# Weights times values of the samples' attention: f32 matmuls against float32r matmuls of split operands

## The chip, the cores and the metric

The kernel runs on one core of a Trainium2 chip. The metric is the device time of one execution in microseconds, as the median of several runs; lower is better. Before the change it is 2456.01 us (three runs, 2455.13 to 2456.61). One further execution was taken by the hardware profiler; the views below are of that one.

The core has five engines that run their own instruction queues in order and wait for each other through semaphores: TensorE (PE, matmuls and transposes; PEld is its loading of the stationary operand), VectorE (DVE), ScalarE (ACT), GpSimd (POOL) and SyncE (SP, which here only issues transfers). Matmul results go to PSUM, everything else lies in SBUF or in HBM.

## What is computed

One layer of a hybrid decoder, for a prompt of 512 tokens and for 8 samples with 4 new tokens each. Both go through a wide input projection, an mLSTM branch, a sliding-window attention branch, a gated merge and a layer norm. The change touches only the attention of the samples, in the reference:

```python
def _swa_sample(q, k_new, v_new, k_buf, v_buf, slopes, sinks):
    k_all = jnp.concatenate([k_buf.astype(k_new.dtype), k_new], axis=1)
    v_all = jnp.concatenate([v_buf.astype(v_new.dtype), v_new], axis=1)
    ...
    out = _sink_attend(q, k_all, v_all, dist, valid, slopes, sinks)
...
# in _sink_attend
    p = jax.nn.softmax(jnp.concatenate([s, sink], axis=-1), axis=-1)[..., :-1]
    return jnp.einsum('...hgqk,...khd->...qhgd', p.astype(v.dtype), v)
```

For each sample there are 128 old keys and values and 4 new ones, 4 key/value heads of 64 and 32 query heads. So for one sample the weights are a matrix of 128 rows (32 heads times 4 tokens) by 132 keys, and the last einsum multiplies them by the values, 128 + 4 rows of 4 x 64 columns.

## The kernel before

**The main work.** The kernel is a long row of matrix products of weights with the 544 tokens (512 of the prompt, 32 of the samples). In the stretch around the change the function paired does them: two column blocks of 128 at a time, in seven steps (half_product, lines 686 to 696), each of 24 float32r matmuls with 272 columns, about 3 us. A product of f32 accuracy is made of three float32r ones: the operand is split into a high part, which is the value rounded to float32r, and a low part, the rest; then high times high, high times low and low times high are added up in PSUM. For the weights, split (lines 202 to 211) makes the high half wh by a cast on ScalarE (L208) and the low half wl by a subtraction on VectorE (L209); there are two buffers of each, and paired prepares them some steps ahead. Sums of raw weights that the seven-step scheme needs come from VectorE as well (L674), and gather (L698 to 723) takes the finished banks out of PSUM.

**The side work.** Everything else is written as generators. After each step tick() lets every live generator run to its next yield, so its instructions are placed between two steps of the main work. The order on each engine comes from a scheduler that simulates the instructions' times at build time (schedule_with_timeline_sim); tc.issue_after pins an instruction behind another one on its engine, and high_priority moves the weight splits ahead.

**The samples' attention** is such a generator, sample_attention (L983 to 1115). It runs after the prompt's attention and before the samples' mLSTM heads, one yield for a step:

- Tiles are taken from the pools t1 and t2 (L984 to 996), with one buffer for each tag. A tile whose tag is used again waits until all uses of the earlier one are over.
- Loads on SyncE's queue: the queries qraw, the new keys kas, the old keys kb (1 MB, L1003), then the new values vas (32 rows of 256, L1007), the old values vb (1 MB, L1008), and the gates gas (L1015). VectorE scales the queries into qas (L1012).
- keysT (L1017 to 1026) turns the old keys on TensorE (L1022) and ScalarE copies them to the tiles with the tags kT0 and kT1 (L1024). The score matmuls (L1039, L1040) follow, then VectorE adds the bias into E (L1042, L1044), and ScalarE takes the exponentials (L1052). E holds for each sample 128 rows by 128 + 4 weights.
- The 4 weights of the new tokens are copied to En (L1059), a tile that GpSimd has set to zero (L995), so that sample b has 32 columns there of which only its own four are filled. En for one sample, turned, is 32 rows (all samples' new tokens) by 128, and fits vas, which holds the new values of all 32 tokens.
- weightsT (L1063 to 1076) turns, for two samples at a time, E (L1068) and En (L1069) on TensorE; ScalarE copies the first (L1073), VectorE the second (L1074), into a tile PT of plain f32.
- values_of (L1078 to 1101) multiplies: for each of the two samples a matmul of PT with vb (L1083, 128 rows) and one of the 32 rows with vas (L1084), both plain f32, both 256 columns into the same PSUM region. VectorE then scales the rows into O (L1090), TensorE turns O (L1095), and VectorE multiplies by the gates (L1101). Four such groups run, the weights of the next one being turned right after the matmuls of the one before (L1103 to 1112).

Of the kernel before, what the change touches and what calls it, by code (L numbers as in the profile page):

```python
# [15 lines left out]
F32 = mybir.dt.float32  # L16
F32R = mybir.dt.float32r
AF = mybir.ActivationFunctionType
ALU = mybir.AluOpType

D = 2048
SEQ = 512
NB = 8
NTS = 4
NS = NB * NTS
T = SEQ + NS
# [5 lines left out]
GRP = 8  # L32
# [42 lines left out]
def _build(tc, nc, i, o, es):  # L75
# [12 lines left out]
    V, A, G, PE = nc.vector, nc.scalar, nc.gpsimd, nc.tensor  # L88
# [16 lines left out]
    def nm(s):  # L105
        count[0] += 1
        return f"{s}_{count[0]}"
# [9 lines left out]
    def r32(ap):  # L117
        return ap.bitcast(F32)
# [33 lines left out]
    ident = cc[:, C_ID:C_ID + 128]  # L152
# [20 lines left out]
    d_vr = dr.tile([T, 256], F32, name="d_vr")  # L173
# [136 lines left out]
    for c0, n in ((0, 256), (256, 256), (512, 512), (1024, 512), (1536, 512)):  # L310
        if c0 < 1536:
            t_ = xr.tile([128, 4, n], F32, tag=f"x{n}", name=nm("xr"))[:]
        else:
            t_ = act2.tile([128, 8, HT], F32, tag="act", name=nm("xr"))[:].rearrange("p a b -> p (a b)")
            t_ = blk(t_[:, 0:4 * n])
# [16 lines left out]
    for g in range(8):  # L332
        for q in range(2):
            k = g * 2 + q
            pt = sm()
# [11 lines left out]
            else:  # L347
                hilo(pt[:], xk2[0][k // 4 - 2][:, k % 4, 0:SEQ], xk2[1][k // 4 - 2][:, k % 4, 0:SEQ])
                x_cast = state["x_cast"]
                c = (slice(None), k - 8, slice(0, SEQ - HT))  # L350
                state["x_end"] = V.tensor_tensor(out=s1r[c], in0=pt[:, HT:SEQ], in1=s1r[c], op=ALU.subtract)
        if g % 2:
# [8 lines left out]
            else:  # L361
                hilo(src, *(xk2[p][g // 2 - 2][:, :, SEQ:T] for p in range(2)))
                c = (slice(None), slice(k4.start - 8, k4.stop - 8), slice(SEQ - HT, HT))
# [619 lines left out]
    def sample_attention():  # L983
        t1, t2 = pool(esT, "t1", 1), pool(esT, "t2", 1)  # L984
        gas = t1.tile([128, 16, NS], F32, name="gas")
        qraw = t1.tile([128, 2, GRP, NS], F32, name="qraw")
        qas = t1.tile([128, 2, NB, GRP, NTS], F32, name="qas")
        kas = t1.tile([128, 2, NS], F32, name="kas")
        vas = t1.tile([32, 256], F32, name="vas")
        kb = t1.tile([128, NB, 256], F32, name="kb")  # L990
        vb = t1.tile([128, NB, 256], F32, name="vb")
        E = t1.tile([128, NB, 132], F32, name="E")

        En = t1.tile([128, 9 * NS], F32, name="En")
        G.memset(En[:], 0.0)  # L995
        st = t1.tile([128, 4, NB], F32, name="sast")
        def buffer_load(t_, src):
            nc.sync.dma_start(t_[:], i[src].rearrange("b t k d -> t b (k d)"))

        with tc.issue_after(state["load"].ins):  # L1000
            nc.sync.dma_start(qraw[:], d_qa[:])
            nc.sync.dma_start(kas[:], d_ka[:, :, SEQ:T].rearrange("k p t -> p k t"))
            buffer_load(kb, "state_attn_k")  # L1003
        yield
        yield
        with tc.issue_after(state["load"].ins):
            nc.sync.dma_start(vas[:], d_vr[SEQ:T])  # L1007
            buffer_load(vb, "state_attn_v")  # L1008
        yield
        with tc.issue_after(state["split"].ins):  # L1010
            for j in range(2):
                V.tensor_scalar(qas[:, j], qraw[:, j].rearrange("p g (b t) -> p b g t", t=NTS), 0.125, None, op0=ALU.mult)  # L1012
        yield
        with tc.issue_after(state["load"].ins):
            nc.sync.dma_start(gas[:], d_bra[:, :, SEQ:T].rearrange("k p t -> p k t"))  # L1015

        def keysT(b2_):  # L1017
            kTs = []
            for bb in range(2):
                pk = sm()  # L1020
                for kk in range(2):
                    PE.transpose(pk[:, kk * 128:kk * 128 + 128], kb[:, b2_ * 2 + bb, kk * 128:kk * 128 + 128], ident)  # L1022
                kT = t1.tile([128, 2, 128], F32, tag=f"kT{bb}", name=nm("kT"))
                A.copy(kT[:].rearrange("p a b -> p (a b)"), pk[:, 0:256])  # L1024
                kTs.append(kT)
            return kTs

        kTs = keysT(0)
        for b2_ in range(4):
            yield  # L1030
            ps_, pn_ = sm(), sm()
            for bb in range(2):
                b = b2_ * 2 + bb
                for kvh in range(KVH):
                    r = slice((kvh % 2) * 64, (kvh % 2) * 64 + 64)
                    q = qas[r, kvh // 2, b].rearrange("p g t -> p (g t)")
                    orow = slice(kvh * 32, kvh * 32 + 32)
                    tp = ((kvh % 2) * 64, kvh * 32)
                    PE.matmul(ps_[orow, bb * 128:bb * 128 + 128], q, kTs[bb][r, kvh // 2], start=True, stop=True, tile_position=tp)  # L1039
                    PE.matmul(pn_[orow, bb * 4:bb * 4 + 4], q, kas[r, kvh // 2, b * 4:b * 4 + 4], start=True, stop=True, tile_position=tp)  # L1040
            sl = slice(b2_ * 2, b2_ * 2 + 2)
            V.tensor_tensor(out=E[:, sl, 0:128], in0=blk(ps_[:, 0:256], 2),  # L1042
                            in1=state["ca"][:, 256:384].unsqueeze(1).to_broadcast([128, 2, 128]), op=ALU.add)
            V.tensor_tensor(out=E[:, sl, 128:132], in0=blk(pn_[:, 0:8], 2),  # L1044
                            in1=state["ca"][:, 384:388].unsqueeze(1).to_broadcast([128, 2, 4]), op=ALU.add)
            if b2_ < 3:
                kTs = keysT(b2_ + 1)
        V.tensor_reduce(st[:, 0], E[:], mybir.AxisListType.X, ALU.max)
        V.tensor_scalar(st[:, 0], st[:, 0], sinkc[:], -1.0, op0=ALU.max, op1=ALU.mult)
        for b in range(NB):  # L1050
            with tc.issue_after(state["cast"].ins):
                A.activation(E[:, b], E[:, b], AF.Exp, bias=st[:, 0, b:b + 1], accum_out=st[:, 1, b:b + 1])  # L1052
            if b % 2:
                yield
        V.tensor_scalar(st[:, 2], st[:, 0], sinkc[:], None, op0=ALU.add)
        A.activation(st[:, 2], st[:, 2], AF.Exp)
        V.tensor_tensor(out=st[:, 1], in0=st[:, 1], in1=st[:, 2], op=ALU.add)
        V.reciprocal(st[:, 1], st[:, 1])
        V.tensor_copy(En[:].rearrange("p (b x) -> p b x", x=NS + NTS)[:, :, 0:NTS], E[:, :, 128:132])  # L1059
        for _ in range(3):  # L1060
            yield

        def weightsT(b2_):  # L1063
            PTs = []
            for bb in range(2):
                b = b2_ * 2 + bb
                pt = sm()
                PE.transpose(pt[:, 0:128], E[:, b, 0:128], ident)  # L1068
                PE.transpose(pt[:32, 128:256], En[:, b * NS:b * NS + NS], ident)  # L1069

                p_, t_ = (t1, "kT") if b2_ % 2 else (t2, "PT")
                PT = p_.tile([128, 2, 128], F32, tag=f"{t_}{bb}", name=nm("PT"))
                A.copy(PT[:, 0], pt[:, 0:128])  # L1073
                V.tensor_copy(PT[:32, 1], pt[:32, 128:256])  # L1074
                PTs.append(PT)
            return PTs

        def values_of(b2_, PTs):  # L1078

            po = sm()  # L1080
            for bb in range(2):
                c = slice(bb * 256, bb * 256 + 256)
                PE.matmul(po[:, c], PTs[bb][:, 0], vb[:, b2_ * 2 + bb], start=True, stop=False)  # L1083
                PE.matmul(po[:, c], PTs[bb][:32, 1], vas[:], start=False, stop=True)  # L1084
            yield
            O = t2.tile([128, 2, HD], F32, tag="O", name=nm("O"))
            rs = st[:, 1, b2_ * 2:b2_ * 2 + 2]
            for kvh in range(KVH):
                r = slice(kvh * 32, kvh * 32 + 32)
                V.tensor_tensor(out=O[r], in0=blk(po[r], 2)[:, :, kvh * HD:kvh * HD + HD],  # L1090
                                in1=rs[r].unsqueeze(2).to_broadcast([32, 2, HD]), op=ALU.mult)
            yield
            yield
            pt = sm()
            PE.transpose(pt[:, 0:128], O[:].rearrange("p b d -> p (b d)"), ident)  # L1095
            for bb in range(2):
                t0 = (b2_ * 2 + bb) * NTS
                src = pt[bb * 64:bb * 64 + 64, 0:128].rearrange("p (k a t) -> p k a t", a=2, t=NTS)
                for a in range(2):
                    gv = gas[a * 64:a * 64 + 64, :, t0:t0 + NTS]  # L1100
                    V.tensor_tensor(out=gv, in0=src[:, :, a], in1=gv, op=ALU.mult)  # L1101

        PTs = weightsT(0)  # L1103
        before = iter(())
        for b2_ in range(4):
            yield
            for _ in before:
                yield
            before = values_of(b2_, PTs)
            next(before)  # L1110
            if b2_ < 3:
                PTs = weightsT(b2_ + 1)
        for _ in before:
            yield
        nc.sync.dma_start(d_bra[:, :, SEQ:T].rearrange("k p t -> p k t"), gas[:])
# [1056 lines left out]
```

## Time and profile before

| | |
|---|---|
| median of the timed runs | 2456.01 us |
| span of the profiled execution | 2451.8 us, 49001 instructions |
| granted TensorE clock, mean over the span | 0.999 |
| samples' attention, first load to last store | about 911.7 to 1007.3 us |
| L1083, f32 matmuls with vb | 16 records, 379 ns median |
| L1084, f32 matmuls with vas | 16 records, 426 ns median |
| L1068 and L1069, the turning of E and En | 8 records each, 273 and 272 ns |

A record of an f32 matmul is one of two that the instruction is made of, so 16 records are 8 matmuls. Matmuls are pipelined: one starts before the one ahead of it has ended, and what a matmul costs is read from the distance between starts, not from its duration. The views quoted below are the page, the busy time by stretch, the timeline (start, duration, engine, line, names, shapes, count; in brackets the idle time before it and what ended it) and the groups of instructions by line.

### The profile page before, as it was taken

What the parts mean: (1) busy time and instruction counts of PE and PEld (TensorE: products, weight loads), DVE (VectorE), ACT (ScalarE), POOL (GpSimd) and SP (SyncE); (2) the same over time, 40 slices, a digit from 0 to 9 for tenths busy, and PEclk for the clock granted to TensorE, in tenths of its full rate; (3) what the DMA queues carried; (4) which work ended last, traced back from release to release, by engine and by line L of the source; (5) the groups of instructions that cost most, each with busy time, mean ns of one, the idle gap of its engine ahead of it and who ended that gap; (6) DMA issues with size and microseconds to landing.
All of it is one profiled execution on the core that took longest, in us unless ns stands there. A gap on an engine that the chain in (4) does not pass through costs nothing.

```text
span 2451.8 us, 49001 instructions
## 1 busy us (share of the span) xinstructions
PE 2435.9 (99%) x19394; PEld 2375.0 (97%) x19394; DVE 1904.6 (78%) x2855; ACT 1250.1 (51%) x2069; POOL 524.6 (21%) x504
## 2 busy tenths in 40 slices
PE   9999999999999999999999999999999999999999
PEld 8999999999999999999999999999999999999997
DVE  7778888888888887887877888887766676877666
ACT  6466676676666665443433444444644444434432
POOL 4114334333333330211111121111000120111111
PEclk9999999999999999999999999999999999999999
DMA  6876666766767754577687676676865598898776
GB/s 181 202 174 156 162 162 145 164 159 166 175 167 182 168 149 126 146 225 228 194 254 231 176 232 220 184 240 214 254 180 190 168 254 241 232 235 271 200 220 197
DMA packets 569405, 479.55 MB, mean 196 GB/s; under 512 B 48600, under 2 KB 464136, under 8 KB 568920
## 3 DMA queue, kind: packets, MB, share of 16 engines
q1 hardware_dynamic: 550424, 410.63, 56.7%
q0 software_dynamic: 17840, 64.23, 13.4%
q8 instruction: 152, 2.49, 0.4%
q10 hardware_dynamic: 912, 1.57, 0.2%
q14 instruction: 77, 0.63, 0.1%
HBM read 326.29 MB, written 100.77 MB: 174 GB/s over the span
## 4 chain that ended last, share of the span: by engine, by line
PE 96%; DMA 1%; DVE 1%; ACT 0%; issue 0%; SPq 0%; DVEq 0%; ACTq 0%
PE bank L694 48%; PE bank L696 24%; PE bank L218 10%; PE sm L1504 2%; PE sm L218 2%; PE bank L1311 1%; PE sm L1538 1%; PE sm L809 1%; PE sm L1554 1%; PE sm L860 1%; PE sm L1993 1%; PE sm L835 1%; PE sm L1316 1%; DVE wl L209 0%; DMA xr<-in_x_prompt 0%; PE bank L418 0%
## 5 line engine op out<-in xcount | busy, mean ns | idle before, releaser
L208 ACT CAST wh<-raw 128x1024 fp32r<-128x1024 f32 x641 | 672.2, 1049 | 833.3 <-PE bank L694 715.3
L209 DVE TENSOR_TENSOR wl<-raw,wh 128x1024 fp32r<-128x1024 f32 x641 | 802.2, 1252 | 209.2 <-ACT wh L208 184.9
L694 PE MATMUL bank<-xk,wh 128*128 128x272 f32 x2336 | 323.1, 289 | 0.0
L674 DVE TENSOR_TENSOR raw<-raw,raw 128x1024 f32<-128x1024 f32 x244 | 309.6, 1270 | 6.6 <-DMA raw<-in_w_in 1.3
L694 PEld LDWEIGHTS bank<-xk,wh 128*128 128x128 f32 x2336 | 303.2, 188 | 2.0 <-issue 1.5
L713 POOL TENSOR_TENSOR ev<-p,ev 128x272 f32<-128x272 f32 x85 | 116.8, 1374 | 460.6 <-ACT ev L712 419.2
L696 PE MATMUL bank<-xk,wl 128*128 128x272 f32 x1168 | 170.0, 287 | 0.0
L694 PE MATMUL bank<-n2h,wh 128*128 128x272 f32 x656 | 169.9, 291 | 0.0
L694 PE MATMUL bank<-n3h,wh 128*128 128x272 f32 x656 | 169.3, 290 | 0.6 <-DVE ev L715 0.4
L694 PE MATMUL bank<-s1h,wh 128*128 128x272 f32 x656 | 169.7, 291 | 0.0
L694 PE MATMUL bank<-n2l,wh 128*128 128x272 f32 x656 | 167.8, 287 | 0.0
L694 PE MATMUL bank<-n3l,wh 128*128 128x272 f32 x656 | 167.7, 288 | 0.0
L694 PE MATMUL bank<-s4h,wh 128*128 128x272 f32 x656 | 167.6, 289 | 0.0
L694 PE MATMUL bank<-s1l,wh 128*128 128x272 f32 x656 | 167.3, 287 | 0.0
L694 PE MATMUL bank<-s4l,wh 128*128 128x272 f32 x656 | 167.0, 287 | 0.0
L696 PEld LDWEIGHTS bank<-xk,wl 128*128 128x128 f32 x1168 | 155.6, 188 | 0.1
L694 PE MATMUL bank<-a11h,wh 128*128 128x272 f32 x584 | 150.3, 289 | 0.0
L672 POOL DMA_DIRECT2D raw<-raw x96 | 83.3, 868 | 311.9 <-DVE ev L721 217.0
L694 PE MATMUL bank<-a11l,wh 128*128 128x272 f32 x584 | 149.5, 288 | 0.0
L694 PEld LDWEIGHTS bank<-n3h,wh 128*128 128x128 f32 x656 | 123.4, 188 | 2.1 <-issue 1.0
L694 PEld LDWEIGHTS bank<-s1h,wh 128*128 128x128 f32 x656 | 123.2, 188 | 1.6 <-issue 1.0
L694 PEld LDWEIGHTS bank<-n2h,wh 128*128 128x128 f32 x656 | 123.3, 188 | 1.4 <-issue 1.4
(537 smaller groups left out, 5789.0 us busy)
## 6 DMA issues: line engine op xcount, KB each, us to landing
raw<-in_w_in SPq DMA_DIRECT2D x296, 512.0 KB
raw<-raw POOLq DMA_DIRECT2D x96, 512.0 KB, 5.0
C<-in_state_mlstm_C SPq DMA_DIRECT2D x32, 1024.0 KB
out<-C SPq DMA_DIRECT2D x64, 512.0 KB
raw<-in_w_proj_a SPq DMA_DIRECT2D x32, 512.0 KB
raw<-in_w_proj_m SPq DMA_DIRECT2D x32, 512.0 KB
raw<-in_w_out SPq DMA_DIRECT2D x32, 512.0 KB
d_v<-ev SPq DMA_DIRECT2D x16, 272.0 KB
```

The lines of the kernel that those rows point to most:

```text
L208: state["cast"] = A.copy(wh[:, k:k + n], raw[:, k:k + n])
L209: state["split"] = V.tensor_tensor(out=wl[:, k:k + n], in0=raw[:, k:k + n], in1=r32(wh[:, k:k + n]), op=ALU.subtract)
L218: PE.matmul(ps[f][:, :w], a[:, kk], b(k, c, w), start=(k == 0 and n == 0), stop=(k == 15 and n == 2))
L672: G.dma_start(out=w[out][:], in_=w[b][:], accum_op=ALU.add)
L674: V.tensor_tensor(out=w[out][:], in0=w[a][:], in1=w[b][:], op=ALU.add)
L694: PE.matmul(ps, wh[:, k], x(p, k), start=(first and k == 0 and p == 0), stop=False, skip_group_check=True)
L696: state["end"] = PE.matmul(ps, wl[:, k], x(0, k), start=False, stop=(k == 7), skip_group_check=True)
L713: G.tensor_tensor(out=c22, in0=p1, in1=c11, op=ALU.subtract)
L809: PE.matmul(pp[:, c0 + w0:c0 + 256], qs[a][:, j * 128:j * 128 + 128], kx[:, k0:k0 + 256 - w0], start=(n == 0), stop=(n == 1))
L835: PE.transpose(pt[:, b * 128:b * 128 + 128], s_[:, b, 128:256], ident)
L860: PE.matmul(po[:, b * 128:b * 128 + n], VA[:, b], p_[:, 2 * b:2 * b + n // 128], start=(b == 0 and m == 0), stop=(b == 3 and m == 1), skip ...
L1504: state["cells"] = PE.matmul(pp[:, 0:258], a[:, b * 128:b * 128 + 128], b_[:, b, f], start=(b == 0 and n == 0), stop=(b == 3 and n == 2))
```

## The change

- The eight plain f32 matmul pairs become float32r ones. The weights of the old keys are split on the way out of PSUM into PT[:, 0] (high, ScalarE's copy) and PT[:, 1] (low, VectorE); the old values are split into vh (high, four ScalarE copies, in the place of kb) and vl (low, VectorE, two samples at a time, in the place of qas). Three matmuls of 128 rows take the place of L1083.
- For the new tokens the three terms are stacked along the contraction: En has three copies of a sample's 32 columns, so its turned form has 96 rows; PN holds high, high and low parts of the weights in rows 0 to 31, 32 to 63 and 64 to 95, and vas holds high, low and high parts of the values. One matmul of 96 rows takes the place of L1084.
- The new values are loaded three times, into a tile vraw that has the tag kT0, from which VectorE makes vas, one copy and one subtraction. PT is placed in the tags qraw (even groups) and kT0, kT1 (odd groups). En grows from 9 x 32 to 24 x 32 columns, and is filled by four copies instead of one.

```diff
+        vraw = t1.tile([128, 2, 128], F32, tag="kT0", name="vraw")[:96].rearrange("p a b -> p (a b)")
+        vas = t1.tile([96, 256], F32R, name="vas")
...
-            nc.sync.dma_start(vas[:], d_vr[SEQ:T])
+            for r in range(3):
+                nc.sync.dma_start(vraw[r * 32:r * 32 + 32], d_vr[SEQ:T])
             buffer_load(vb, "state_attn_v")
         yield
         with tc.issue_after(state["split"].ins):
             for j in range(2):
                 V.tensor_scalar(qas[:, j], qraw[:, j].rearrange("p g (b t) -> p b g t", t=NTS), 0.125, None, op0=ALU.mult)
+            V.tensor_copy(vas[:], vraw)
+            V.tensor_tensor(out=vas[32:64], in0=vraw[32:64], in1=r32(vas[32:64]), op=ALU.subtract)
...
-        V.tensor_copy(En[:].rearrange("p (b x) -> p b x", x=NS + NTS)[:, :, 0:NTS], E[:, :, 128:132])
+        for r in range(0, 96, NS):
+            V.tensor_copy(En[:, 0:7 * (96 + NTS)].rearrange("p (b x) -> p b x", x=96 + NTS)[:, :, r:r + NTS], E[:, 0:7, 128:132])
+        V.tensor_copy(En[:, 672:768].rearrange("p (r x) -> p r x", x=NS)[:, :, NS - NTS:NS],
+                      E[:, 7, 128:132].unsqueeze(1).to_broadcast([128, 3, NTS]))
...
         def weightsT(b2_):
             PTs = []
+            vl = t1.tile([128, 2, 256], F32R, tag="qas", name=nm("vl"))
+            pair = slice(b2_ * 2, b2_ * 2 + 2)
+            V.tensor_tensor(out=vl[:], in0=vb[:, pair], in1=r32(vh[:, pair]), op=ALU.subtract)
+            both = None if b2_ % 2 else t1.tile([128, 2, 2, 128], F32R, tag="qraw", name=nm("PT"))
...
-                PE.transpose(pt[:32, 128:256], En[:, b * NS:b * NS + NS], ident)
-
-                p_, t_ = (t1, "kT") if b2_ % 2 else (t2, "PT")
-                PT = p_.tile([128, 2, 128], F32, tag=f"{t_}{bb}", name=nm("PT"))
+                PE.transpose(pt[:96, 128:256], En[:, b * 96:b * 96 + 96], ident)
+
+                PT = t1.tile([128, 2, 128], F32R, tag=f"kT{bb}", name=nm("PT")) if b2_ % 2 else both[:, bb]
+                PN = t2.tile([96, 128], F32R, tag=f"PN{b2_ % 2}{bb}", name=nm("PN"))
                 A.copy(PT[:, 0], pt[:, 0:128])
-                V.tensor_copy(PT[:32, 1], pt[:32, 128:256])
-                PTs.append(PT)
+                V.tensor_tensor(out=PT[:, 1], in0=pt[:, 0:128], in1=r32(PT[:, 0]), op=ALU.subtract)
+                V.tensor_copy(PN[:], pt[:96, 128:256])
+                V.tensor_tensor(out=PN[64:96], in0=pt[64:96, 128:256], in1=r32(PN[64:96]), op=ALU.subtract)
+                PTs.append((PT, PN, vl[:, bb]))
...
-                PE.matmul(po[:, c], PTs[bb][:, 0], vb[:, b2_ * 2 + bb], start=True, stop=False)
-                PE.matmul(po[:, c], PTs[bb][:32, 1], vas[:], start=False, stop=True)
+                P, vl = PTs[bb][0], PTs[bb][2]
+                for n, (a, v_) in enumerate(((P[:, 0], vh[:, b2_ * 2 + bb]), (P[:, 1], vh[:, b2_ * 2 + bb]), (P[:, 0], vl))):
+                    PE.matmul(po[:, c], a, v_, start=n == 0, stop=False)
+                PE.matmul(po[:, c], PTs[bb][1][:], vas[:], start=False, stop=True)
...
+        vh = t1.tile([128, NB, 256], F32R, tag="kb", name="vh")
+        for b in range(0, NB, 2):
+            A.copy(vh[:, b:b + 2], vb[:, b:b + 2])
         PTs = weightsT(0)
```

More of the change, by code (lines that the diff above doesn't have):

```diff
@@ L985, in sample_attention @@
         gas = t1.tile([128, 16, NS], F32, name="gas")
-        qraw = t1.tile([128, 2, GRP, NS], F32, name="qraw")
-        qas = t1.tile([128, 2, NB, GRP, NTS], F32, name="qas")
+        qraw = t1.tile([128, 2, GRP, NS], F32, tag="qraw", name="qraw")
+        qas = t1.tile([128, 2, NB, GRP, NTS], F32, tag="qas", name="qas")
         kas = t1.tile([128, 2, NS], F32, name="kas")
-        vas = t1.tile([32, 256], F32, name="vas")
-        kb = t1.tile([128, NB, 256], F32, name="kb")
+        vraw = t1.tile([128, 2, 128], F32, tag="kT0", name="vraw")[:96].rearrange("p a b -> p (a b)")
+        vas = t1.tile([96, 256], F32R, name="vas")
+        kb = t1.tile([128, NB, 256], F32, tag="kb", name="kb")
         vb = t1.tile([128, NB, 256], F32, name="vb")
         E = t1.tile([128, NB, 132], F32, name="E")
-        En = t1.tile([128, 9 * NS], F32, name="En")
+        En = t1.tile([128, 24 * NS], F32, name="En")
         G.memset(En[:], 0.0)
```

## Prediction

> **What bounds the kernel now.** I read the page first, then the busy time in stretches around the samples' attention, then the order of TensorE's and VectorE's instructions there.
>
> ```profile
> span 2451.8 us, 49001 instructions
> ## 1 busy us (share of the span) xinstructions
> PE 2435.9 (99%) x19394; PEld 2375.0 (97%) x19394; DVE 1904.6 (78%) x2855; ACT 1250.1 (51%) x2069; POOL 524.6 (21%) x504
> PE 96%; DMA 1%; DVE 1%; ACT 0%; issue 0%; SPq 0%; DVEq 0%; ACTq 0%
> ```
>
> TensorE (PE) is busy 99% of the span and carries 96% of the chain that ended last. A matmul record is longer than the distance to the next one, so "busy" alone can hide small waits; prices below are therefore distances between starts. As long as TensorE's queue has no hole, a microsecond of matmul time that goes is a microsecond of the end, and work of other engines costs nothing until TensorE waits for it. The profiled execution lasted 2451.8 us and the median of the timed runs is 2456.0, so 4.2 us lie around the span. I take them as unchanged.
>
> The edited code runs from about 912 to 1007 us. These are the stretches (columns: the length; busy time and count on each engine; granted clock; DMA):
>
> ```profile
> core 0: us, PE busy (x) PEld busy (x) DVE busy (x) ACT busy (x) POOL busy (x), PEclk, DMA share, GB/s
> 890.00:915.00 25.00, 25.00 (x204) 25.00 (x203) 24.06 (x25) 13.47 (x18) 12.51 (x9) 1.00 0.41 112
> 955.00:980.00 25.00, 25.00 (x181) 22.35 (x180) 17.89 (x32) 11.51 (x19) 2.78 (x2) 1.00 0.36 96
> 980.00:1010.00 30.00, 30.00 (x219) 27.32 (x218) 23.75 (x42) 11.38 (x16) 2.80 (x2) 1.00 0.35 89
> ```
>
> TensorE has no hole there and its granted clock is 1.00, so the stage is bound by matmul work. VectorE is at 41.6 of 55 us from 955 to 1010. The first row matters later: just before this stage VectorE was busy 24.06 of 25 us and TensorE still had no hole.
>
> **The matmuls that go.** values_of issues, for each of eight samples, one plain-f32 matmul of 128 rows (L1083) and one of 32 rows (L1084), 256 columns each. They come in four groups. The first group and the ends of the last one in TensorE's order (start, duration, line; each f32 matmul is two records, hence x2):
>
> ```profile
> 959.56 0.59 PE L1083 MATMUL sm<-vb,PT 128*128 128x256 f32 x2
> 959.99 0.27 PE L1068 MATMUL sm<-cc,E 128*128 128x128 f32 x1
> ...
> 962.05 0.69 PE L1084 MATMUL sm<-vas,PT 32*128 32x256 f32 x2
> 962.67 0.70 PE L1083 MATMUL sm<-vb,PT 128*128 128x256 f32 x2
> 963.30 0.69 PE L1084 MATMUL sm<-vas,PT 32*128 32x256 f32 x2
> 963.92 0.33 PE L1068 MATMUL sm<-cc,E 128*128 128x128 f32 x1
> ...
> 995.63 0.59 PE L1083 MATMUL sm<-vb,PT 128*128 128x256 f32 x2
> ...
> 998.03 2.28 PE L694 MATMUL bank<-xk,wh 128*128 128x272 f32 x16
> ```
>
> Group one takes 0.43 + 1.87 = 2.30 us, the last 998.03 - 995.63 = 2.40, and the two between them have the last one's form, so the four take 2.30 + 3 x 2.40 = 9.5 us. Something lies at the edges too: the transpose that follows group one has a record of 0.33 us where the one at 959.99 has 0.27. I add 0.06 for each group's end, 0.2 in all: **9.7 us go**. One f32 matmul in the middle of a group costs 0.62 to 0.63, alone ahead of another kind 0.43.
>
> **The matmuls that come.** 24 of 128 rows and 8 of 96 rows, all float32r, 256 columns: 32 matmuls. Two neighbours price them, attention's (L860, of each eight six with 256 columns and two with 128) and the projection's (L696, 272 columns):
>
> ```profile
> 895.62 1.16 PE L696 MATMUL bank<-xk,wl 128*128 128x272 f32 x8
> 896.62 1.04 PE L860 MATMUL sm<-P,VA 128*128 128x256 f32 x8
> 897.50 0.34 PE L694 MATMUL bank<-n3h,wh 128*128 128x272 f32 x1
> ```
>
> Eight L860 take 0.88 us, 0.110 each, a lower bound since two are short. Eight L696 take 1.00 us, 0.125 each, an upper bound since they are wider. By width, 0.125 x 256/272 = 0.118. The 96-row ones get the same price: L1084 with 32 rows is no shorter above than L1083 with 128. So 32 x 0.118 = 3.8 us (3.5 to 4.0). The transpose of the new weights now has 96 columns of stationary operand and still 128 moving ones: nothing. TensorE's balance is 9.7 - 3.8 = **5.9 us less** (5.5 to 6.2).
>
> A rule of the Trainium skill gives less. FP8 and Floating Point Precision, section TensorE Precision Notes, says that a true FP32 matmul makes four passes through the array; at 0.118 us a pass the sixteen would cost 7.6 us, and the balance would be 3.8. The isolated L1083 (0.43 us) agrees with it, the ones inside a group (0.62) do not, and the measured rows decide.
>
> **VectorE.** Prices first (start, duration, line, shapes), and below them two rows of the grouped view of 905 to 1010 us (count, busy us and mean ns of one, idle time before):
>
> ```profile
> 916.21 0.50 DVE L1012 TENSOR_SCALAR qas<-qraw 128x256 f32<-128x256 f32 x2 [0.90 <-DMA qraw<-d_qa]
> 916.62 1.22 DVE L674 TENSOR_TENSOR raw<-raw,raw 128x1024 f32<-128x1024 f32 x1
> 917.76 0.44 DVE L715 SCALAR_TENSOR_TENSOR ev<-bank,p 128x272 f32<-128x272 f32 x1
> 918.11 1.22 DVE L209 TENSOR_TENSOR wl<-raw,wh 128x1024 fp32r<-128x1024 f32 x1
> 921.54 1.23 DVE L209 TENSOR_TENSOR wl<-raw,wh 128x1024 fp32r<-128x1024 f32 x1 [2.21 <-ACT kT L1024]
> 924.84 0.43 DVE L1042 TENSOR_TENSOR E<-sm,ca 128x256 f32<-128x256 f32 x1 [2.08 <-PE sm L1040]
> ```
>
> ```profile
> L1090 DVE TENSOR_TENSOR O<-sm,sast 32x128 f32<-32x128 f32 x16 | 4.6, 287 | 3.0 <-PE sm L1084 2.8
> ...
> L1024 ACT COPY kT<-sm 128x256 f32<-128x256 f32 x8 | 2.6, 376 | 2.8 <-PE sm L1022 2.8
> ```
>
> In weightsT: four vl subtractions of 128x512 at half of L209 and a little, 0.65, 2.6 us; eight low parts PT[:,1] of 128x128, between L1090's 0.29 (the same 128 elements a partition) and L1042's 0.43 (256) and nearer the former, 0.30, 2.4 us; eight low parts PN of 32x128 at L1090's 0.29, 2.3 us; the PN copy only replaces L1074 with more partitions. That is 7.3 us. Outside it the vas copy and subtraction (256 elements wide, about 0.3 each) and three more small copies into En (0.2 each) make 1.2 us. From 955 to 1010 VectorE would have 41.6 + 7.3 = 48.9 us of work for the 55 - 5.9 = 49.1 us that TensorE still needs. That is full, and only the lead hides it: a low weight half is ready some 4 us before its use (L209 at 918.11 ends at 919.33 and is used from 923.28, in a row below). A deficit would have to eat that lead first, and 24.06 of 25 without a hole has just been seen. I cost it at nothing, with up to 3 us if the cover fails (a deficit of that size after the lead is used up).
>
> The first group is tighter: transpose, ScalarE copy, low part, two PN steps and vl(0) must all pass VectorE within the one tick between weightsT(0) and values_of(0), behind weight splits of 1.22 us. I take 0.5 us of waiting (none to 1.5, about one split).
>
> **ScalarE and GpSimd.** Four copies of vb into vh, 128x512; L1024 in the row above needs 0.38 for 256 columns, so 0.65 each, 2.6 us together. ScalarE was busy 11.51 of 25 us in the stretch above, so its idle time hides them; without it a cast queued behind all four would be 2.6 us late, inside the lead of a weight half. GpSimd's memset of En is 768 wide instead of 288, on an engine that is 2.78 of 25 busy.
>
> **The three loads and a new wait.** The new tokens' values are now loaded three times, and into a tile that shares its place with kT0. So VectorE must copy and subtract them before ScalarE may write kT0. On SyncE's queue:
>
> ```profile
> 912.71 0.46 SPq L998 DMA_DIRECT2D kb<-in_state_attn_k  x1
> 913.22 1.15 SPq L1007 DMA_DIRECT2D vas<-d_vr  x1
> 914.41 0.43 SPq L998 DMA_DIRECT2D vb<-in_state_attn_v  x1
> 914.94 2.88 SPq L1365 DMA_DIRECT2D d_g<-ev  x1
> ```
>
> Two more issues are 0.9 to 2.3 us of SyncE's time (0.43 or 1.15 each). The next store stands at the queue for 2.88 us anyway, so most of it vanishes there; 64 KB more is 0.2 to 0.3 us of transfer. TensorE waited 1.1 us for kb, until 920.68; vraw is issued behind kb, so I expect it at 921 to 922. If the copy into vas stands in VectorE's queue right behind L1012 (916.7), VectorE stops until then, and L674, L715 and L209 (2.7 us of work up to 919.33) wait behind it. TensorE's use of those halves:
>
> ```profile
> 920.68 0.63 PE L1022 MATMUL sm<-cc,kb 128*128 128x128 f32 x4 [1.14 <-DMA kb<-in_state_attn_k]
> ...
> 923.28 0.79 PE L696 MATMUL bank<-n3h,wl 128*128 128x272 f32 x5
> 924.00 0.44 PE L1039 MATMUL sm<-kT,qas 64*32 64x128 f32 x8
> ```
>
> VectorE would be free at about 922.2 (landing 921.6, two steps of 0.3), the half of 918.11 done at 925.0 instead of 919.33, and its use at 923.28 would slip by 1.7 us. kT0 would be copied by 922.9, still ahead of L1039 at 924.00. If the copy stands behind those three instead, it falls into VectorE's hole of 2.21 us and costs nothing on TensorE. Both ends stay; I take nothing, because the three have to be done first for TensorE and the order is made from estimated landing times.
>
> **Sum.** 5.9 less on TensorE, 0.5 back at the first group: 5.4 us. Span 2446.4, time 2456.0 - 5.4 = **2450.6 us**, 0.22% less. This measurement tells about 0.2% (4.9 us) from no change, so the forecast stands just beyond that line (2451.1).
>
> **The rivals.**
> - *vraw stops VectorE* (above): for it, kb's late landing and L1012's own wait of 0.90; against it, the hole at 919.33. It gives 1.7 to 2.5 us back: 2452.3 to 2453.1, no change that can be told.
> - *VectorE becomes the bound of the value groups*: for it, 48.9 us of work in 49.1; against it, the stretch of 24.06 in 25. It costs 1 to 3 us: 2451.6 to 2453.6.
> - *The new matmuls pay for changing weights as the f32 ones do*: inside a group an f32 record pair costs 0.62 against 0.43 alone, 0.10 per record. With 0.10 on each of 32 the new groups cost 7.0, the balance is 2.7 and the time 2453.8. Against it: L860 also changes weights with each matmul or every second one, and pays nothing.
> - *Slower: vraw lands behind everything that is queued.* Place: the same VectorE wait. If vraw came only after vb (another 1 MB, some 6 us by kb's 8 us from 912.71 to 920.68), at 928, VectorE's three instructions would end at 931.3 and the use at 923.28 slip by 8 us; kT0 would hold TensorE at L1039 likewise. Less 5.9 that is 2 to 3 us slower, 2458 to 2459, and past 2460.9 if raw loads got ahead as well. The landing from which it is a loss is about 925.4. Against it: vraw is issued before vb.
>
> **How the numbers follow.** Forecast case 0.55 (2449.4 to 2451.6, of which 0.50 lies below 2451.1), vraw 0.20, VectorE 0.10, weights 0.05, late vraw 0.06 (half of it past 2460.9), the order of instructions changed elsewhere 0.04 (0.01 faster, 0.01 within, 0.02 slower). Faster 0.51, within 0.2% 0.44, slower 0.05. The range goes from the full balance of 6.2 with the edges dearer still (2449.0) to the dearest ends of the vraw, VectorE and weight cases with something added (2455.0).
>
> **What would show it.** Right: four value groups of about 0.95 us each on TensorE, 0.118 between starts; no new hole of TensorE between 915 and 930; VectorE above 90% from 955 to 1005. Wrong: starts 0.2 apart inside a group; TensorE waiting for wl, kT or PT; VectorE idle for vraw with L674 behind it. A difference that arises outside 910 to 1010 us would mean that the order changed elsewhere, which no row here prices.

## The result and the profile after

| | before | after |
|---|---|---|
| median | 2455.60 us (17 runs, 2452.56 to 2456.81) | 2451.82 us (17 runs, 2448.22 to 2453.55) |
| span of the profiled execution | 2451.8 us | 2451.1 us |
| ratio | | 0.9986, 95% interval 0.998 to 0.9993 |

The ratio is 3.4 us of 2455.6, with an interval of 1.7 to 4.9. A second series of the same two kernels gave 2455.44 and 2448.31 us, ratio 0.9975 (0.9967 to 0.9984), which is 6.1 us (3.9 to 8.1). The forecast of 5.4 us lies inside the second interval and just beyond the first. The experiments below come in three sets, each on another chip and with its own series of before, and each ratio is taken within its set. Single executions of one kernel spread over 4 to 8 us (one of before in the second series, 2607.34 us at a granted clock of 0.85, stands apart and is in no ratio), and the two spans above differ by 0.7 us only; most of what follows is about why.

The page of the changed kernel, the lines that answer to those of before:

```profile
span 2451.1 us, 49031 instructions
## 1 busy us (share of the span) xinstructions
PE 2433.0 (99%) x19394; PEld 2376.7 (97%) x19394; DVE 1910.1 (78%) x2880; ACT 1251.4 (51%) x2073; POOL 524.4 (21%) x504
...
PE 94%; DVE 2%; DMA 2%; issue 1%; ACT 1%; SPq 0%; POOL 0%; POOLq 0%; DVEq 0%; ACTq 0%
```

TensorE is 2.9 us less busy, and carries 94% of the chain that ended last instead of 96%: more of the end is now decided by waits.

The stretch of the samples' attention (columns as in the prediction's table):

```profile
core 0: us, PE busy (x) PEld busy (x) DVE busy (x) ACT busy (x) POOL busy (x), PEclk, DMA share, GB/s
955.00:1010.00 55.00, 55.00 (x445) 54.87 (x444) 52.95 (x98) 26.08 (x39) 6.70 (x4) 1.00 0.47 118
```

TensorE still has no hole there, with VectorE at 52.95 of 55 us. The second of the four groups, in TensorE's timeline:

```profile
970.22 0.27 PE L1110 MATMUL sm<-cc,O 128*128 128x128 f32 x1
970.25 0.48 PE L1098 MATMUL sm<-vh,PT 128*128 128x256 f32 x2
970.57 0.28 PE L1098 MATMUL sm<-vl,PT 128*128 128x256 f32 x1
970.68 0.28 PE L1099 MATMUL sm<-vas,PN 96*128 96x256 f32 x1
970.80 0.40 PE L1098 MATMUL sm<-vh,PT 128*128 128x256 f32 x2
971.04 0.28 PE L1098 MATMUL sm<-vl,PT 128*128 128x256 f32 x1
971.16 0.28 PE L1099 MATMUL sm<-vas,PN 96*128 96x256 f32 x1
971.28 0.27 PE L1079 MATMUL sm<-cc,E 128*128 128x128 f32 x1
```

Eight matmuls from 970.25 to 971.28 (1.03 us, 0.08 of it the tail of the transpose ahead), where the f32 group took 2.40. The starts are 0.12 apart, also across the step from 128 rows to 96.

The best measure of the gain takes the executions' spread out. The main work's matmuls (L694, L696, L218) are the same 16632 in each kernel, in the same order but for at most 172 places, so the start of each can be subtracted from that of its twin in the trace of before. The table gives this shift for the matmuls that stand at 940 and 1009 us there, so that only the value groups lie between, for all kernels of this study:

| kernel | shift at 940 | at 1009 | gain between |
|---|---|---|---|
| before, second trace | +0.36 | +0.36 | 0.00 |
| before with one more step (before_slack) | -0.98 | -0.98 | 0.00 |
| after | +0.27 | -5.64 | 5.91 |
| after, second trace | +1.00 | -4.91 | 5.91 |
| after_slack, two traces | -0.94, -0.56 | -6.87, -6.47 | 5.93, 5.91 |
| only_old | +0.28 | -0.36 | 0.64 |
| only_new | +0.88 | -4.64 | 5.52 |
| pad128 | -0.92 | -3.89 | 2.97 |
| new32 | -1.09 | -1.53 | 0.43 |
| dve_more | +1.87 | -2.37 | 4.24 |

A minus is a start ahead of its twin in before. **The value groups give 5.91 us in each of four traces of the changed groups and 0.00 in the other traces of before.** The shift at 940 is what differs between executions ahead of the change, in the first loads and in the wait for kb.

Where it went in the first pair of traces: at 1560 us the changed kernel is still 5.64 us ahead, at 1616 us 2.83, at 2166 us 1.86, and at the end 0.7. The last 1.2 us go between the issue of the last store and the end of the span (3.8 us in the changed kernel, 2.6 before), and most of the step of 0.97 is a halt of TensorE at 2122 us for a low half (s1l) that VectorE makes. The large step is one wait of TensorE, for the values VB of the last mLSTM head, which the samples' work writes to HBM (d_kv) and loads again. Before (first fence) and after (second) in TensorE's timeline:

```profile
1579.27 0.51 PE L1316 MATMUL sm<-VB,Ab 32*128 32x512 f32 x4 [1.32 <-DMA VB<-d_kv]
1579.71 0.39 PE L694 MATMUL bank<-n2h,wh 128*128 128x272 f32 x1
1579.94 0.29 PE L694 MATMUL bank<-n2l,wh 128*128 128x272 f32 x1
1580.06 0.29 PE L694 MATMUL bank<-n2h,wh 128*128 128x272 f32 x1
```

```profile
1574.90 0.51 PE L1334 MATMUL sm<-VB,Ab 32*128 32x512 f32 x4 [2.59 <-DMA VB<-d_kv]
...
1576.28 0.43 PE L694 MATMUL bank<-n2h,wh 128*128 128x272 f32 x1
1576.50 0.43 PE L694 MATMUL bank<-n2l,wh 128*128 128x272 f32 x1
1576.73 0.43 PE L694 MATMUL bank<-n2h,wh 128*128 128x272 f32 x1
```

The wait is 1.27 us longer, and behind it the starts are 0.225 us apart instead of 0.125 for 3.4 us: the granted clock fell to half, which the view by stretch shows as a mean of 0.91 where before had 1.00:

```profile
1566.00:1586.00 20.00, 17.41 (x127) 16.11 (x126) 12.26 (x18) 8.22 (x11) 5.85 (x7) 0.91 0.63 176
```

That adds 1.5 us. Is it tied to the change, or chance?

### The profile page after: what moved, and what is told of

It is laid out like the page before. It is cut to its first block, busy times and chain, and to the rows that moved or that the text cites. A ratio compares the mean times of both kernels' runs of the same rounds, so it can differ in the third digit from the quotient of the medians.

```text
span 2451.1 us, 49031 instructions
## 1 busy us (share of the span) xinstructions
PE 2433.0 (99%) x19394; PEld 2376.7 (97%) x19394; DVE 1910.1 (78%) x2880; ACT 1251.4 (51%) x2073; POOL 524.4 (21%) x504
## 4 chain that ended last, share of the span: by engine, by line
PE 94%; DVE 2%; DMA 2%; issue 1%; ACT 1%; SPq 0%; POOL 0%; POOLq 0%; DVEq 0%; ACTq 0%
PE bank L694 47%; PE bank L696 23%; PE bank L218 9%; PE sm L1522 2%; PE sm L218 2%; PE bank L1329 1%; PE sm L1556 1%; PE sm L1572 1%; PE sm L809 1%; PE sm L860 1%; PE sm L2011 1%; DVE wl L209 1%; PE sm L1334 1%; PE sm L835 1%; DMA xr<-in_x_prompt 0%
## 5 line engine op out<-in xcount | busy, mean ns | idle before, releaser
L694 PE MATMUL bank<-xk,wh 128*128 128x272 f32 x2336 | 323.1, 289 | 0.0
L694 PEld LDWEIGHTS bank<-xk,wh 128*128 128x128 f32 x2336 | 303.2, 188 | 1.7 <-issue 1.2
L694 PE MATMUL bank<-n2h,wh 128*128 128x272 f32 x656 | 171.0, 292 | 0.0
L696 PE MATMUL bank<-xk,wl 128*128 128x272 f32 x1168 | 170.0, 287 | 0.0
L694 PE MATMUL bank<-n3h,wh 128*128 128x272 f32 x656 | 169.4, 290 | 0.3 <-ACT wh L208 0.2
L694 PE MATMUL bank<-s1h,wh 128*128 128x272 f32 x656 | 169.6, 291 | 0.0
L694 PE MATMUL bank<-n2l,wh 128*128 128x272 f32 x656 | 169.0, 289 | 0.0
L694 PE MATMUL bank<-s1l,wh 128*128 128x272 f32 x656 | 167.5, 287 | 0.5 <-DVE s1l L255 0.5
L694 PE MATMUL bank<-n3l,wh 128*128 128x272 f32 x656 | 167.6, 288 | 0.0
L694 PE MATMUL bank<-s4h,wh 128*128 128x272 f32 x656 | 167.6, 289 | 0.0
L694 PE MATMUL bank<-s4l,wh 128*128 128x272 f32 x656 | 167.0, 287 | 0.0
L696 PEld LDWEIGHTS bank<-xk,wl 128*128 128x128 f32 x1168 | 155.6, 188 | 0.1
L694 PE MATMUL bank<-a11h,wh 128*128 128x272 f32 x584 | 150.3, 289 | 0.0
L694 PE MATMUL bank<-a11l,wh 128*128 128x272 f32 x584 | 149.5, 288 | 0.0
L694 PEld LDWEIGHTS bank<-n2h,wh 128*128 128x128 f32 x656 | 124.0, 189 | 1.4 <-issue 1.4
L694 PEld LDWEIGHTS bank<-n3h,wh 128*128 128x128 f32 x656 | 123.4, 188 | 2.0 <-issue 1.2
L694 PEld LDWEIGHTS bank<-s1h,wh 128*128 128x128 f32 x656 | 123.2, 188 | 1.6 <-issue 1.0
```

What stands on the lines that cost most here:

```text
L694: PE.matmul(ps, wh[:, k], x(p, k), start=(first and k == 0 and p == 0), stop=False, skip_group_check=True)
L696: state["end"] = PE.matmul(ps, wl[:, k], x(0, k), start=False, stop=(k == 7), skip_group_check=True)
```

## The experiments

### Second traces of both kernels

**after_again**: the changed kernel, nothing edited.

> The changed kernel once more, for a second trace. Theory 1 (TensorE gains 6.1 us in the samples' attention in every execution, and what is given back is lost at TensorE's wait for VB of the last mLSTM head and in the stretch of half clock behind a wait of over 2 us): the four value groups again cost 3.7 to 3.9 us, the shift against the trace of before is again -6.0 to -6.2 us across 915 to 1010 us, and the wait for VB is again over 2 us with matmul starts 0.225 us apart behind it. Rival (that wait is chance, of one execution): wait between 0 and 1.5 us, no half clock there, span 2.8 us shorter. Time against before: -3 to -4.5 us by both.

2448.31 us (11 runs, 2445.84 to 2452.38), 6.1 us below before by the ratio, where both theories had 3 to 4.5. The groups' gain was 5.91 us (table), a little under the expected 6.0. Its wait for VB was 1.7 us, between the two theories, with no half clock behind it.

**before_again**: the kernel before, nothing edited.

> The kernel before once more, for a second trace. Theory 1: the wait for VB is again 1.0 to 1.6 us and no half clock follows it. Rival (chance): anything from 0 to 3 us, as in the changed kernel. The four groups of f32 matmuls again cost 9.5 us between their first and last starts.

2455.45 us (one run). Its wait for VB was 2.4 us, without half clock either; from the list of TensorE's waits (total, times, longest):

```profile
PE sm L1316 <- DMA VB<-d_kv: 2.4, 1, 2.4
```

So theory 1 falls in its claim that the long wait belongs to the changed kernel: 1.3 and 2.4 us before, 2.6 and 1.7 after. Counting the partial kernels below, nine traces have this wait, from 1.3 to 2.8 us, and in three of them (waits of 2.6, 2.2 and 2.8 us) the half clock follows and costs another 1.5 us. The length differs from execution to execution, which is a part of their spread; what sets it, no run shows.

Whether half clock follows is not decided by the length of the wait alone: 2.4 us in before_again had none behind it, 2.2 in only_old had. In all twelve traces each stretch of half clock up to 2400 us lasts 3.41 us, and within a trace these stretches start whole multiples of 3.413 us apart (after: 1576.08 and 1770.64, which is 57 of them). Cut along these multiples, the wait of after lies mostly in one stretch (first fence), that of before_again across two (second):

```profile
1572.67:1576.08 3.41, 1.18 (x10) 0.94 (x11) 0.68 (x2) 0.00 (x0) 0.69 (x1) 1.00 0.96 254
1576.08:1579.49 3.41, 3.41 (x18) 3.41 (x17) 3.21 (x5) 0.71 (x1) 0.09 (x1) 0.50 0.20 41
```

```profile
1576.29:1579.70 3.41, 2.01 (x17) 0.95 (x15) 1.33 (x2) 1.36 (x2) 0.76 (x4) 1.00 0.64 154
1579.70:1583.11 3.41, 2.38 (x19) 2.15 (x20) 1.85 (x3) 0.00 (x0) 0.77 (x1) 1.00 0.69 190
```

In after, TensorE is idle for 2.23 us of the first stretch (3.41 less 1.18 busy), and the next is at half clock (0.50). In before_again it is idle for 1.40 and 1.03 us, and the clock stays at 1.00. The other traces fit: from the first matmul to 2400 us, every stretch with 2.22 us or more of idle time is followed by one of half clock, and none with 1.70 us or less; between these two values there is no stretch.

### One step more before VB is used

```diff
-            for j in range(5 if h + b == 0 else 4 + b % 2):
+            for j in range(5 if b == 0 and h in (0, MH - 1) else 4 + b % 2):
```

The last head then yields once more between the load of VB and the matmuls that need it.

> The changed kernel, with one more step of the main work between the load of KB and VB of the last mLSTM head and their first use. Theory 1: the wait for VB and the half clock behind it are gone, TensorE gains 2.5 to 3 us there, and the time is 6 to 7 us below before (2449 against 2455.6). Rival (the wait swallows nothing that would not be lost elsewhere, since the work behind it waits for the same transfers): the wait goes, the time stays within 1 us of the changed kernel's, 3 to 4.5 us below before.

> The kernel before with the same additional step. Theory 1: TensorE gains the 1.3 us of its wait for VB, no more, so the time is 1 to 1.5 us below before, and after_slack is 5.2 to 6.1 us below this one, the full gain of the value groups. Rival: no change against before (within 0.5 us), and after_slack 3 to 4.5 us below it.

| | median | ratio to before |
|---|---|---|
| before_slack | 2452.80 us (11 runs) | 0.9992 (0.9983 to 1.0002) |
| after_slack | 2445.99 us (5 runs, 2444.98 to 2447.48) | 0.9966 (0.9953 to 0.9979) |
| after_slack_2 | 2446.13 us (5 runs, 2444.38 to 2449.91) | 0.9965 (0.9952 to 0.9977) |

The wait is gone from all three traces, and the stretch around it runs at full clock, here in after_slack:

```profile
1560.00:1580.00 20.00, 20.00 (x159) 18.68 (x160) 17.01 (x25) 9.77 (x14) 8.23 (x7) 1.00 0.59 159
```

By medians the step gives 2.6 us in the kernel before (expected 1 to 1.5; its interval just includes no change) and 2.3 in the changed one, which now lies 9.4 us below before by medians, where 6 to 7 were expected. These times alone do not settle it, since the intervals of the changed kernel with and without the step overlap. The traces do: before_slack is 0.98 us ahead of before at 1560 us and 2.48 at 2000, and keeps that to 2400. The gain of 1.5 us is theory 1's, and the rival, that the time would be lost elsewhere, is refuted. Without the wait the two kernels are 6.8 us apart by medians (expected 5.2 to 6.1), and the traces of before_slack and after_slack 5.9 to 6.0 us from 1009 to 2400 us.

> The changed kernel with one more step before the last head's first use of VB, a second time: 2445 to 2447 us, 8 to 10 us below before, no wait for VB and no half clock near 1570 us in its trace.

The second series of the changed kernel with this step agrees: 8.1 us below its own before (2454.25 us), without the wait. These two series are the fastest of the study. After_slack_2 gains another 1.2 us on after_slack near 1770 us. There, in every trace, TensorE waits 2.9 to 3.2 us at L218 for VectorE. In eleven of the twelve, half clock follows. In after_slack_2 the wait falls into two stretches, 1.64 and 1.26 us, and none follows.

### Each half of the change alone

**only_old**: the old keys' product is split, the new tokens stay as they were. The edit to the changed kernel, at its core:

```diff
-        vas = t1.tile([96, 256], F32R, name="vas")
+        vas = t1.tile([32, 256], F32, name="vas")
...
-                V.tensor_copy(PN[:], pt[:96, 128:256])
-                V.tensor_tensor(out=PN[64:96], in0=pt[64:96, 128:256], in1=r32(PN[64:96]), op=ALU.subtract)
+                V.tensor_copy(PN[:], pt[:32, 128:256])
```

> Only the old keys' product is split (24 float32r matmuls); the new tokens keep their eight f32 matmuls of 32 rows, which now stand between float32r ones. Theory A (an f32 matmul costs 0.43 us, and 0.62 only where it follows or precedes another f32 one with other weights): the groups cost 24 x 0.118 + 8 x 0.43 = 6.3 us, 3.4 less than before's 9.7. Theory B (0.62 is the price wherever it stands): 2.8 + 8 x 0.62 = 7.8 us, 1.9 less. Read from the shift of the main work's matmuls from 915 to 1010 us against the trace of before; the time follows with the executions' spread of 2 to 3 us.

**only_new**: the 96-row matmul stays, the old keys go back to one f32 matmul of PT and vb, without vh, vl and low parts of PT.

```diff
-                for n, (a, v_) in enumerate(((P[:, 0], vh[:, b2_ * 2 + bb]), (P[:, 1], vh[:, b2_ * 2 + bb]), (P[:, 0], vl))):
-                    PE.matmul(po[:, c], a, v_, start=n == 0, stop=False)
+                PE.matmul(po[:, c], PTs[bb][0][:, 0], vb[:, b2_ * 2 + bb], start=True, stop=False)
```

> Only the new tokens' product is stacked (8 float32r matmuls of 96 rows); the old keys keep their eight f32 matmuls, which now stand between float32r ones, and VectorE and ScalarE have no vl, vh and PT low parts to make. Theory A: 8 x 0.43 + 8 x 0.118 = 4.4 us, 5.3 less than before, within 0.8 us of the whole change. Theory B: 8 x 0.62 + 0.9 = 5.9 us, 3.8 less.

| | median | ratio to before | gain of the groups |
|---|---|---|---|
| only_old | 2454.94 us (11 runs) | 0.9998 (0.9989 to 1.0006) | 0.64 us |
| only_new | 2451.76 us (11 runs) | 0.9981 (0.9972 to 0.9990) | 5.52 us |

Neither theory holds for only_old, which gains less than B's 1.9; only_new is A's 5.3 or a little more. One sample of each, in TensorE's timeline, shows why. only_old:

```profile
983.81 0.28 PE L1090 MATMUL sm<-vl,PT 128*128 128x256 f32 x1
984.02 0.69 PE L1091 MATMUL sm<-vas,PN 32*128 32x256 f32 x2
984.64 0.50 PE L1090 MATMUL sm<-vh,PT 128*128 128x256 f32 x2
984.98 0.27 PE L1090 MATMUL sm<-vl,PT 128*128 128x256 f32 x1
```

only_new:

```profile
981.74 0.60 PE L1092 MATMUL sm<-vb,PT 128*128 128x256 f32 x2
981.98 0.47 PE L1093 MATMUL sm<-vas,PN 96*128 96x256 f32 x1
982.29 0.60 PE L1092 MATMUL sm<-vb,PT 128*128 128x256 f32 x2
```

In only_old the f32 matmul of 32 rows costs 0.62 between float32r neighbours too, and they pay with it: the vl matmul ahead takes 0.21 instead of 0.12, the two behind 0.34 instead of 0.24. In only_new an f32 matmul of 128 rows and its float32r neighbour of 96 take 0.55 together, which is 0.43 + 0.12. What turns 0.43 into 0.62 is thus not f32 beside f32 but, it seems, the 32 rows.

### Rows or number format

**pad128**: the kernel before, all f32, with the new tokens' matmul padded with zeros to 128 rows.

```diff
-        vas = t1.tile([32, 256], F32, name="vas")
+        vas = t1.tile([128, 256], F32, name="vas")
...
-                PE.matmul(po[:, c], PTs[bb][:32, 1], vas[:], start=False, stop=True)
+                PE.matmul(po[:, c], PTs[bb][:, 1], vas[:], start=False, stop=True)
```

> The kernel before, all in f32, but the new tokens' matmul has 128 rows (the 96 rows beyond its own are zero on both sides) instead of 32; PT of the even groups lies in qraw's place, as in the changed kernel. Theory C (what makes an f32 matmul of the groups dear is the change between 128 and 32 contraction rows, about 0.1 us at each such edge): 16 x 0.43 = 6.9 us instead of 9.7, a shift of -2.6 to -3.0 us across 915 to 1010 us. Rival D (two f32 matmuls with different weights behind each other cost 0.62 each, whatever the rows): 9.7 us, shift 0.

**new32**: the changed kernel, with three float32r matmuls of 32 rows for the new tokens.

```diff
-                PE.matmul(po[:, c], PTs[bb][1][:], vas[:], start=False, stop=True)
+                for n, (h_, v_) in enumerate(((0, 0), (0, 1), (1, 0))):
+                    PE.matmul(po[:, c], PTs[bb][1][:, h_], vas[:, v_], start=False, stop=n == 2)
```

> The changed kernel with the new tokens' three terms as three float32r matmuls of 32 rows instead of one of 96 rows. Theory C: 48 x 0.118 = 5.7 us and two edges of about 0.1 us for each of eight samples, 7.3 us, a shift of -2.4 us (-2.0 to -2.8) across the stretch. Rival D (the surcharge belongs to f32): 5.7 us, shift -4.0 to -4.4.

pad128's third group in TensorE's timeline:

```profile
981.23 0.60 PE L1084 MATMUL sm<-vb,PT 128*128 128x256 f32 x2
981.66 0.59 PE L1085 MATMUL sm<-vas,PT 128*128 128x256 f32 x2
982.09 0.59 PE L1084 MATMUL sm<-vb,PT 128*128 128x256 f32 x2
982.52 0.59 PE L1085 MATMUL sm<-vas,PT 128*128 128x256 f32 x2
982.95 0.27 PE L1070 MATMUL sm<-cc,E 128*128 128x128 f32 x1
```

Every f32 matmul costs 0.43 as soon as all have 128 rows, f32 beside f32 with other weights each time: 1.72 for the group instead of 2.40, and 2.97 us gained with four times the rows. new32, one sample:

```profile
982.95 0.29 PE L1094 MATMUL sm<-vl,PT 128*128 128x256 f32 x1
983.16 0.61 PE L1096 MATMUL sm<-vas,PN 32*128 32x256 f32 x3
983.71 0.51 PE L1094 MATMUL sm<-vh,PT 128*128 128x256 f32 x2
984.05 0.29 PE L1094 MATMUL sm<-vl,PT 128*128 128x256 f32 x1
```

Three matmuls take 0.55 instead of 0.36, the one ahead 0.21 instead of 0.12, the pair behind 0.34 instead of 0.24. The single starts in the trace place the surcharge: the three 32-row matmuls take 0.224, 0.116 and 0.203 us, the vl matmul ahead 0.216, the first one behind 0.223. The one in the middle, with 32 rows on both sides, costs no more than a 128-row one (0.118), so it is the change of rows that costs, about 0.1 us on each side of it: some 0.2 us at each of the two edges, twice what theory C had. The gain is 0.43 us instead of its 2.4: three groups gain 0.32 each, and the first, which the main work cuts into pieces with edges of their own, loses 0.5. So theory C had the cause but not the size, which came out in pad128 only (2.97, expected 2.6 to 3.0); rival D is refuted by both. Times: pad128 2452.77 us, ratio 0.9991 (0.9982 to 1.0); new32 2455.46 us, 0.9999 (0.999 to 1.0008).

### More work for VectorE

```diff
-            V.tensor_tensor(out=vl[:], in0=vb[:, pair], in1=r32(vh[:, pair]), op=ALU.subtract)
+            for _ in range(3):
+                V.tensor_tensor(out=vl[:], in0=vb[:, pair], in1=r32(vh[:, pair]), op=ALU.subtract)
```

> The changed kernel with each of the four vl subtractions made three times, 8 x 0.69 = 5.5 us more on VectorE, which is already busy 53 of the 55 us from 955 to 1010. Theory 1 (the lead of the weight halves hides VectorE until a deficit exceeds some 3 to 4 us): 53 + 5.5 = 58.5 us of work, 3.5 us more than fits, so TensorE has holes of 0 to 2 us behind wl in this stretch, and the time rises by 0 to 2 us over the changed kernel's. Rival (VectorE is the bound there already, and each microsecond more costs one): holes of 5 us or more, time up by 5 us.

2452.62 us (11 runs), ratio 0.9985 (0.9976 to 0.9994), by medians 0.8 us above the changed kernel's first series and 4.3 above its second. The groups' gain falls from 5.91 to 4.24, so 5.5 us of work cost 1.7 on TensorE, within theory 1's 0 to 2, and the rival's 5 or more are refuted. Its largest hole:

```profile
980.91 1.37 PE L694 MATMUL bank<-xk,wh 128*128 128x272 f32 x9 [1.40 <-DVE ev L719]
```

It is a bank that VectorE had not yet emptied (L719), not a weight half: the cover that ends first is another than the prediction named. With two series of the changed kernel so far apart, the medians say no more than that.

## Why the prediction was right, and what it had wrong

- **TensorE's balance, 5.9 us: right**, 5.91 in four traces. 32 matmuls at 0.118 came 0.12 us apart in the group shown, the 96-row ones among them. The price of what went was read correctly from the rows, without its cause.
- **Why the f32 groups were dear: not seen.** The gap is in the sentence that L1084 with 32 rows is no shorter than L1083 with 128. True, but those 32 rows were what made both cost 0.62. pad128 takes half of the gain (2.97) with f32 alone. The other half is 16 f32 matmuls at 0.43 (6.9) against 32 float32r ones at 0.12 (3.8). The rival that the new matmuls would pay for changing weights had the cause wrong as well: they change weights each time and pay nothing.
- **The rule of four passes** gave 3.8 us. It prices the f32 matmul of full rows fairly (4 x 0.118 = 0.47 us; 0.43 in pad128), and misses the edges. A passage of the Trainium skill may bear on these: TensorEngine Tiling (Array Packing), section Key Properties, says that changing the tiling mode drains TensorE. The traces agree in so far as 32 rows among 128 cost about 0.3 to 0.4 us for the two edges in new32, and 96 rows nothing; that it is the mode that changes, no run shows.
- **VectorE costs nothing: right.** 52.95 of 55 us without a hole. Of dve_more's 5.5 us more, 1.7 came out as holes of TensorE and 3.8 did not; from how much on it costs anything, no run shows. The cover that ended first there was a bank's, not the lead of the weight halves.
- **0.5 us at the first group: wrong**, nothing was lost there.
- **vraw: right.** VectorE's timeline shows the copy in the hole, with landing at the expected time:

```profile
918.56 1.22 DVE L209 TENSOR_TENSOR wl<-raw,wh 128x1024 fp32r<-128x1024 f32 x1
921.97 0.29 DVE L1015 CAST vas<-vraw 96x256 fp32r<-96x256 f32 x1 [2.19 <-DMA vraw<-d_vr]
922.29 0.41 DVE L1016 TENSOR_TENSOR vas<-vraw,vas 32x256 fp32r<-32x256 f32 x1
922.74 1.22 DVE L209 TENSOR_TENSOR wl<-raw,wh 128x1024 fp32r<-128x1024 f32 x1
```

- **The sum, 5.4 us, against 3.4 and 6.1 in two series.** What failed is that a microsecond of matmul time that goes is a microsecond of the end. It held at the value groups, but a gain at 1000 us meets waits further on, which vary by more than a microsecond from execution to execution: of the 5.64 us in the first pair of traces, 2.8 went at the wait for VB and the half clock behind it, and 2.1 further on. That the first series still came out at 2451.8, near 2450.6, is in part luck: the 0.5 us given back for the first group were not lost there, and stood in for losses that no term named. The likelier of the forecast's outcomes, a time below 2451.1 us, came in the second series only. With the wait for VB removed in both kernels, 6.8 us remain by medians. How much of the difference between the two series is the wait for VB and how much the first loads, no run separates.
- **The span, 2446.4 us, against 2451.1: wrong.** It took 4.2 us between the span and the time as fixed: before_again has 2.0 (2455.45 against 2453.5), after 1.8 (2452.9 against 2451.1). The profiled execution of before was probably a quick one; its own time is not on record. The forecast of the time does not rest on this term.

## What to carry to other kernels

Where a small matmul stands among full ones, look at the distances between starts around it before blaming its number format: stacking terms to 96 rows, or padding with zeros to 128, removed edges that cost almost as much as the matmul itself (0.38 us for each pair of f32 matmuls, against 0.43 for one). Of the two halves of this change the stacking gave 5.5 us and the split of the old keys 0.4 to 0.6, while it took VectorE from 49.55 us (only_new) to 52.95 of the 55. And when a gain is a few tenths of a per cent, measure it in the trace between twin instructions, because one late transfer can hide it.

## What the runs showed of the hardware

- A change between 32 and 128 contraction rows costs about 0.2 us: some 0.1 on the last matmul ahead and 0.1 on the first behind, in float32r (new32, 0.216 and 0.224 us instead of 0.118) and in f32 (before, 0.62 instead of 0.43 for a matmul between two such changes). A matmul of 32 rows between others of 32 costs no more than one of 128 (0.116 us). 96 rows among 128 cost nothing.
- A plain f32 matmul of 128 rows and 256 columns costs 0.43 us, 3.6 times a float32r one (0.12).
- Up to 2400 us the granted clock fell to half, for 3.41 us at a time, behind every stretch of 3.41 us (at multiples that are fixed within a trace) in which TensorE was idle for 2.22 us or more, and behind none with 1.70 us or less; each fall at the wait for VB cost 1.5 us. Near the end of the kernel it also falls without such a wait, which no run explains. TensorE: Matmul & The Clock Gate, of the Trainium skill, section Part 1: The HAM clock gate, gives an idle window of about 3.4 us for this; the traces agree with the length of the window, but 2.2 us of idle time in it were enough.
